# A fused attention layer on one core: the query projection with weights stationary, rotated with head dimensions on partitions, and carried through DRAM

## The chip, the core and the metric

The kernel runs on one core of a Trainium2 chip. Everything is fp32 data. The metric is device time in microseconds (us) of one execution; three runs of the kernel before gave 1683.66, 1688.36 and 1689.98 us, so the median is 1688.36.

## What is computed

One layer of a hybrid network over 1024 latent tokens and 128 context tokens, 1152 in all, with 1024 channels. Of its many parts these matter here:

```
h = rmsnorm(x, g1) * (1 + sc1) + sh1                 # 1152 x 1024
u_f, q, k, v, g = split(h @ w_in)                    # 512 | 1024 | 256 | 256 | 2048 columns
q, k = apply_rope(q), apply_rope(k)                  # latent tokens only; 16 q heads, 4 kv heads, head_dim 64
#   x1, x2 = x[..., 0::2], x[..., 1::2];  out pairs = (x1*c - x2*s, x1*s + x2*c)
scores = q k^T / 8, masked to a +/-128 token window, plus 128 cached context keys and a sink logit
attn_o = softmax(scores) v
x = x + ga1 * merge(fourier(u_f), attn_o, gates(g))  ;  then an MLP of width 4096
```

A product q.k does not change when the 64 head dimensions of both q and k are put in another common order, which is what the change makes use of.

## The kernel before

Tokens are cut into nine tiles of 128 (eight latent, one context). h lies in SBUF transposed, channels on partitions, as two fp32r parts (a rounded high part h_hi and the rest h_lo), eight slices of 128 channels each. Every projection is computed from such parts with three matmuls for each pair of slices, high*high, high*low and low*high (helper `mm3`, L193 to L195), so that the result has nearly fp32 accuracy. Weights come by DMA into a tile `wraw` and are split by ScalarE (L145, high part) and VectorE (L140, the difference).

The order of the work around the change is: the Fourier branch with gate units between its steps; then the projection of k and v for all tiles (`tok_proj_round`, L231 to L233); then the attention stage; then the rest of the layer, which the change does not touch. A **gate unit** (`gate_units`, L463) is filler: 24 matmuls of 128x384 with weights stationary and 384 tokens streaming, one of three token chunks of one of 16 blocks of 128 gate columns, 48 units in all. 16 of them run before the attention stage and 32 in it, one in most steps (`filler`, L488).

The attention stage has 36 steps, four groups g of four heads by nine token tiles i. A step s does this:

- `attention_q` (L674) for the *next* step: 24 matmuls of 128x256 into one PSUM bank `q`, with a token tile of h stationary and 256 columns of w_in streaming. So q has tokens on partitions. VectorE rotates it (`apply_rope`, L600: two products from PSUM at L602 and L605, two sums at L612 and L613) and splits it (L688). TensorE transposes the four heads (L691) into a `ptp` bank, and ScalarE copies them to `qT` (L696), where each head is 128 rows: 64 dimensions of the high part and 64 of the low part.
- `attention_scores` (L699): for each of four heads two matmuls (L712, L713), qT stationary and up to 512 keys streaming, into one of two `s` banks; VectorE masks and takes the maximum (L714); ScalarE exponentiates (L726); VectorE inverts the sum (L734); GpSimd scales (L736).
- `attention_out` (L745) for the step *before*: transposes of the probabilities (L755) into one of two `ptp` banks, a copy and a difference (L760, L140 pl), matmuls with v (L765, L766), and the sum of the two halves (L769 to L772), stored by SP (L773).

GpSimd and ScalarE also run slices of the modulation product meanwhile (L303, L305). PSUM has eight banks: two `mm` for gate units, and in this stage one `q`, two `ptp`, two `s`, one `o`. Each engine executes its queue in order; the order is fixed when the program is built, by a scheduler that works from the program order and its own estimate of times. SP issues nearly all DMAs, in order, and an issue that waits holds up those behind it.

## Time and profile before

| | |
|---|---|
| three runs, us | 1683.66, 1688.36, 1689.98 |
| span of the profiled execution, us | 1688.9 |
| mean granted TensorE clock | 0.995 |
| Fourier and k, v projection with filler gates, roughly | 140 to 246 us |
| attention stage, roughly | 246 to 707 us |
| TensorE busy in the attention stage | 441.98 of 461 us |
| VectorE, ScalarE, GpSimd busy in it | 355.67, 325.73, 206.52 us |

The profiled execution is one of its own; no time but its span is known of it, and that lies 0.5 us above the median of the three runs. A matmul's duration in the profile is from its start to its modelled end, and overlaps the next one: what a matmul takes of TensorE is the distance between the starts of two.

### The profile page before, as it was taken

To read this page: it belongs to the slowest core of one execution; us is meant where nothing else is said; L and a number is where in the kernel's file an instruction comes from. 1 tells how busy PE (TensorE), PEld (TensorE's weight loads), DVE (VectorE), ACT (ScalarE), POOL (GpSimd) and SP (SyncE) were. 2 spreads that over 40 slices of the span, in tenths; PEclk is the share of its full clock that TensorE was granted. 3 is DMA by queue.
4 is the path that set the end of the run, shared out by engine and by line. 5 is a ranking of instruction groups with operands and counts; after the bars stand their busy time and mean duration, and the time that the engine had idled before them with its cause. 6 is when DMAs were issued, how large, how long until landed. Compare 5 with 4: busy or idle time off the path is not lost.

```text
span 1688.9 us, 26480 instructions
## 1 busy us (share of the span) xinstructions
PE 1635.4 (97%) x9101; PEld 1453.2 (86%) x9101; DVE 1181.3 (70%) x2402; ACT 916.0 (54%) x1845; POOL 271.6 (16%) x368
## 2 busy tenths in 40 slices
PE   6999999999999999999999899999999999999998
PEld 5899899999899999889988788888888888888887
DVE  7663257777868787778757966777775588776764
ACT  7743236767767767655436664444443454444542
POOL 1010015444535445300001500000000200000000
PEclk9999999999999999999999999999999999999999
DMA  8341481313322211279655524445446996666751
GB/s 294 120 138 65 137 246 42 95 55 96 89 73 79 87 53 56 91 238 311 191 196 191 162 101 159 155 167 169 164 149 144 321 387 194 199 194 191 248 165 63
DMA packets 202038, 264.92 MB, mean 157 GB/s; under 512 B 29400, under 2 KB 129688, under 8 KB 201904
## 3 DMA queue, kind: packets, MB, share of 16 engines
q1 hardware_dynamic: 193648, 253.27, 46.7%
q0 software_dynamic: 8256, 9.96, 2.3%
q8 instruction: 72, 1.18, 0.3%
q14 instruction: 62, 0.51, 0.1%
HBM read 194.73 MB, written 68.44 MB: 156 GB/s over the span
## 4 chain that ended last, share of the span: by engine, by line
PE 78%; DVE 8%; ACT 4%; DMA 4%; issue 3%; POOL 1%; SPq 0%; DVEq 0%; ACTq 0%; POOLq 0%
PE x L1682 6%; PE x L1683 6%; PE x L1681 6%; PE x L1285 6%; PE x L1287 6%; PE x L1286 6%; PE mm L193 3%; PE mm L194 3%; PE mm L195 3%; PE ptp L755 2%; PE x L195 2%; PE x L194 2%; PE x L193 2%; PE x L231 1%; PE x L232 1%
## 5 line engine op out<-in xcount | busy, mean ns | idle before, releaser
L140 DVE TENSOR_TENSOR wlo<-wraw,whi 128x1024 fp32r<-128x1024 f32 x100 | 125.8, 1260 | 83.7 <-ACT whi L145 83.4
L145 ACT CAST whi<-wraw 128x1024 fp32r<-128x1024 f32 x98 | 102.5, 1050 | 97.7 <-PE x L233 20.5
L1682 PE MATMUL x<-BR 128*128 128x512 f32 (+1 forms) x348 | 132.8, 382 | 0.0
L1683 PE MATMUL x<-BR 128*128 128x512 f32 (+1 forms) x348 | 132.4, 382 | 0.0
L1681 PE MATMUL x<-BR 128*128 128x512 f32 (+1 forms) x348 | 131.3, 382 | 0.0
L736 POOL TENSOR_SCALAR pt<-pt,mx 128x512 f32<-128x512 f32 (+2 forms) x144 | 97.0, 685 | 154.6 <-DVE mx L734 137.8
L726 ACT ACTIVATE pt<-pt,mx 128x513 f32<-128x513 f32 (+2 forms) x144 | 94.7, 661 | 35.7 <-DVE mx L724 35.1
L714 DVE CUSTOM_DVE_ANT_0 pt<-s,mask,sink 128x512 f32<-128x512 f32 (+2 forms) x144 | 94.7, 672 | 23.1 <-PE ptp L755 12.4
L1654 ACT CAST BR<-aa 128x512 fp32r<-128x512 f32 x80 | 49.7, 621 | 104.9 <-issue 46.2
L140 DVE TENSOR_TENSOR pl<-ptp,ph 128x512 fp32r<-128x512 f32 (+1 forms) x136 | 86.0, 640 | 14.4 <-ACT ph L760 13.2
L305 POOL TENSOR_TENSOR macc<-macc,mprod 128x512 f32<-128x512 f32 x70 | 92.1, 1316 | 20.1 <-ACT mprod L303 20.0
L194 PE MATMUL mm<-BR,whi 128*128 128x384 f32 x272 | 92.1, 339 | 0.0
L760 ACT CAST ph<-ptp 128x512 fp32r<-128x512 f32 (+1 forms) x136 | 72.5, 546 | 32.6 <-PE ptp L755 30.9
L193 PE MATMUL mm<-BR,whi 128*128 128x384 f32 x240 | 83.6, 348 | 0.0
L1285 PE MATMUL x<-BR,whi 128*128 128x512 f32 (+2 forms) x204 | 79.2, 388 | 4.1 <-ACT ZR L1309 2.8
L195 PE MATMUL mm<-BR,wlo 128*128 128x384 f32 x240 | 81.2, 338 | 0.0
L755 PE MATMUL ptp<-ident,pt 128*128 128x128 f32 x496 | 75.9, 274 | 2.4 <-ACT qT L696 2.1
L1287 PE MATMUL x<-BR,wlo 128*128 128x512 f32 (+2 forms) x204 | 77.6, 380 | 0.0
L1286 PE MATMUL x<-BR,whi 128*128 128x512 f32 (+2 forms) x204 | 77.5, 380 | 0.0
L140 DVE TENSOR_TENSOR BR<-aa,BR 128x512 fp32r<-128x512 f32 x80 | 54.9, 687 | 31.3 <-ACT BR L1654 30.0
L1681 PEld LDWEIGHTS x<-BR 128*128 128x128 f32 x348 | 65.4, 188 | 13.1
L1682 PEld LDWEIGHTS x<-BR 128*128 128x128 f32 x348 | 65.4, 188 | 12.8
(466 smaller groups left out, 5192.9 us busy)
## 6 DMA issues: line engine op xcount, KB each, us to landing
aa<-hr_d SPq DMA_DIRECT2D x108, 256.0 KB
ab<-in_w_ff_dram SPq DMA_DIRECT2D x108, 256.0 KB
hr_d<-ZR SPq DMA_DIRECT2D x104, 256.0 KB
wraw<-in_w_in_dram SPq DMA_DIRECT2D x40, 512.0 KB
wraw<-in_w_ff_dram SPq DMA_DIRECT2D x34, 512.0 KB
mraw<-in_w_ada_dram SPq DMA_DIRECT2D x96, 128.0 KB
wraw<-in_w_out_dram SPq DMA_DIRECT2D x24, 512.0 KB
z_d<-z SPq DMA_DIRECT2D x48, 192.0 KB
```

Of the source, the lines that this page charges most:

```text
L140: eng.tensor_tensor(dst, raw, hi.bitcast(F32), ALU.subtract)
L145: nc.scalar.copy(hi, raw)
L193: nc.tensor.matmul(out, ah, bh, start=start, stop=False)
L194: nc.tensor.matmul(out, ah, bl, start=False, stop=False)
L195: return nc.tensor.matmul(out, al, bh, start=False, stop=stop).ins
L755: nc.tensor.transpose(pst[:, bi, e, :], pt[:, e, b * P : (b + 1) * P], ident)
L1285: nc.tensor.matmul(po, wh, xh, start=(k == 0 and not cont), stop=False, skip_group_check=cont)
L1286: nc.tensor.matmul(po, wh, xl, start=False, stop=False, skip_group_check=cont)
L1287: nc.tensor.matmul(po, wl, xh, start=False, stop=(k == 3), skip_group_check=cont)
L1681: nc.tensor.matmul(ps, xh, bh, start=start, stop=False, skip_group_check=cont)
L1682: nc.tensor.matmul(ps, xh, bl, start=False, stop=False, skip_group_check=cont)
L1683: nc.tensor.matmul(ps, xl, bh, start=False, stop=stop, skip_group_check=cont)
```

## The change

The q projection is turned round. The columns of w_in for q are reordered on the host so that, in each group of four heads, the 32 even dimensions of the four heads come first (128 columns, e = 0) and the 32 odd ones after them (e = 1). A **q unit** (g, j, e) has the shape of a gate unit: the 128 columns stationary, 384 tokens of chunk j streaming, 24 matmuls of 128x384. So q comes out with dimensions on partitions, and the rotation is between two PSUM results, with tables `ropet` that have dimensions on partitions: two products from the even unit, two from the odd one, a difference and a sum, then a copy (high part) and two differences (low parts). Four tiles (even high, odd high, even low, odd low) of 128x384 are stored to DRAM, and `load_qt` reads them back as `qT` for three token tiles, with even high, odd high, even low and odd low of a head below one another on 128 partitions. k is written with its even and odd dimensions in the same order (host reordering of cache_k; `even_odd` in `k_rope`).

24 q units take the place of the 36 calls of `attention_q`. The six units of group 0 run before the k, v projection; the 18 others go with the 32 gate units into one list `work`, 50 units, of which `fill` hands out an even share in each of 34 steps, after the score matmuls of the step. `qT` for a chunk is asked for three steps ahead. The `q` bank becomes a third `s` bank. The tiles of the k, v evacuation get two buffers each in a pool of their own.

```diff
+    q_d = dp.tile([NG, NJ, 4, P, CH], F32, name="q_d")
-        rope = p1.tile([P, 2, 8, HD], F32, name="rope")
-        nc.sync.dma_start(rope, rope_in)
+        ropet = p1.tile([P, 2, NT], F32, name="ropet")
+        nc.sync.dma_start(ropet, ropet_in)
+        def q_units(g):
+            blk, t = {}, {}
+            for j in range(NJ):
+                for e in range(2):
+                    def emit(j=j, e=e):
+                        if j == 0:
+                            blk[e] = load_w(w_in, 0, KC, OFF_Q + g * 256 + e * P, P)
+                        ps = mmt()
+                        gemm_unit(ps, j, wcols(blk[e], KC), hs)
+                        r = slice(j * CH, (j + 1) * CH)
+                        c, sn = ropet[:, 0, r], ropet[:, 1, r]
+                        v = ps[:, :CH]
+                        tt = nc.vector.tensor_tensor
+                        if e == 0:
+                            for n in range(2):
+                                t[n] = p1.tile([P, CH], F32, tag=f"qt{n}", name=nm("qt"), bufs=1)
+                                tt(t[n], v, (c, sn)[n], ALU.mult)
+                            return
+                        for n in range(2, 4):
+                            t[n] = p1.tile([P, CH], F32, tag=f"qt{n}", name=nm("qt"), bufs=1)
+                            tt(t[n], v, (sn, c)[n - 2], ALU.mult)
+                        tt(t[0], t[0], t[2], ALU.subtract)
+                        tt(t[1], t[1], t[3], ALU.add)
+                        for n in range(2):
+                            hi, lo = t[2 + n].bitcast(F32R), t[n].bitcast(F32R)
+                            nc.scalar.copy(hi, t[n])
+                            sub(nc.vector, lo, t[n], hi)
+                            for part, x in ((n, t[2 + n]), (2 + n, t[n])):
+                                nc.sync.dma_start(q_d[g, j, part], x)
+                    yield emit
+        for f in q_units(0):
+            f()
...
-        def attention_q(g, i, qw):
...
+        def load_qt(g, j):
+            qt = pq.tile([P, 4, CH], F32R, tag="qT", name=nm("qT"), bufs=2)
+            for part in range(4):
+                r = slice(32 * part, 32 * part + 32)
+                nc.sync.dma_start(qt.bitcast(F32)[r], q_d[g, j, part].rearrange("(h r) c -> r h c", h=4))
+            return qt
...
-                    sp = q1.tile([P, 512], F32, tag="s", name=nm("s"), bufs=2)
-                    nc.tensor.matmul(sp[:, :n], qT[:, h, :], kth[:, k0 * P : k0 * P + n], start=True, stop=False)
+                    sp = q1.tile([P, 512], F32, tag="s", name=nm("s"), bufs=3)
+                    qs = qT[:, h, (i % 3) * P : (i % 3 + 1) * P]
+                    nc.tensor.matmul(sp[:, :n], qs, kth[:, k0 * P : k0 * P + n], start=True, stop=False)
...
+        share = -(-len(gates) // NG)
+        for g in range(NG):
+            if g + 1 < NG:
+                fs = list(q_units(g + 1))
+                work += fs[:-1] + [lambda g=g + 1, f=fs[-1]: q_last(g, f)]
+            for _ in range(min(share, len(gates))):
+                work.append(gates.pop(0))
+        total = len(work)
+        def fill(s, after):
+            left = total - min(total, -(-total * s // FILL_AT))
+            with tc.issue_after(after):
+                while len(work) > left:
+                    work.pop(0)()
...
             if pending is not None:
                 attention_out(*pending)
-                if s % SKIP:
-                    filler(1, anchor)
+            fill(s, anchor)
```

Apart from numbers in names, the first 794 rows of TensorE's queue (up to the last gate unit of the Fourier branch) and the last 4165 (from the end of the attention stage on) stay in the same order; between them there are 3072 rows where there were 3397.

The first place is TensorE's queue behind the last gate unit of the Fourier branch. Before, the projection of k and v (`x` banks) follows at once:

```order
L195 MATMUL mm_239_1569<-BT_70,wlo_236_1538 128x384
L231 MATMUL x_248_1632<-whi_246_1628,BR_69 128x512
L232 MATMUL x_248_1632<-wlo_247_1629,BR_69 128x512
L233 MATMUL x_248_1632<-whi_246_1628,BR_69 128x512
L231 MATMUL x_249_1636<-whi_246_1628,BR_69 128x512
```

In the changed kernel there stand the first matmuls of the six q units of group 0 (`mm_244` to `mm_262`; each has 24 rows), and only then the k, v projection:

```order
L197 MATMUL mm_239_1570<-BT_70,wlo_236_1539 128x384
L195 MATMUL mm_244_1619<-BR_69,whi_242_1615 128x384
...
L195 MATMUL mm_250_1654<-BR_69,whi_248_1650 128x384
...
L195 MATMUL mm_253_1693<-BR_69,whi_242_1615 128x384
...
L195 MATMUL mm_262_1790<-BR_69,whi_248_1650 128x384
...
L233 MATMUL x_272_1854<-whi_270_1850,BR_69 128x512
```

144 matmuls have come ahead of the k, v projection, and their products need `ropet`, which is loaded just there.

The second place is TensorE's queue in an early step of the attention stage. Before, the 24 matmuls of the q tile (`q_481`) are laid in ones and threes between score matmuls (`s`), transposes (`ptp`) and output matmuls (`o`), and end in the transposes of q (L691):

```order
L195 MATMUL q_481_2884<-qwh_326_2167,BR_69 128x256
L712 MATMUL s_454_2762<-kth_2155,qT_402_2541 128x512
L713 MATMUL s_454_2762<-ktl_2156,qT_402_2541 128x512
L193 MATMUL q_481_2884<-qwh_326_2167,BT_70 128x256
...
L766 MATMUL o_419_2598<-pl_425_2618,vg_321_2157 128x256
...
L755 MATMUL ptp_432_2646<-ident_82,pt_371_2392 128x128 x4
...
L691 MATMUL ptp_443_2727<-identr_1602,qhl_441_2720 128x128 x4
L193 MATMUL mm_479_2856<-BR_69,whi_477_2852 128x384
```

In the changed kernel a unit (`mm_526`, a q unit) stands as one run of 24 rows, and the attention's own matmuls stand together:

```order
L727 MATMUL s_504_3046<-ktl_2392,qT_359_2421 128x512
L195 MATMUL mm_526_3137<-BR_69,whi_413_2626 128x384
...
L726 MATMUL s_531_3179<-kth_2391,qT_359_2421 128x512
L727 MATMUL s_531_3179<-ktl_2392,qT_359_2421 128x512
L769 MATMUL ptp_479_2909<-ident_83,pt_426_2698 128x128 x2
L779 MATMUL o_469_2874<-ph_471_2880,vg_354_2393 128x256
...
L769 MATMUL ptp_482_2922<-ident_83,pt_426_2698 128x128 x4
...
L779 MATMUL o_478_2908<-ph_480_2914,vg_354_2393 128x256
```

The fine mixture of filler and attention has become runs of the one and of the other.

The third place is VectorE's queue in the same stage of the changed kernel, between two q pairs: the low parts of one pair (`qt_410`, `qt_411`), then the products of the next even unit (`qt_453`, `qt_454`), which are written to the same two buffers, and behind them the drain of a score bank (L728). The waits named DMAHW are for landings of DMAs:

```order
L142 TENSOR_TENSOR qt_410_2620<-qt_410_2620,qt_416_2655 128x384 [waits Activation_49]
...
L142 TENSOR_TENSOR qt_411_2622<-qt_411_2622,qt_417_2657 128x384 [waits Activation_49]
L738 TENSOR_SCALAR mx_427_2699<-mx_427_2699 128x2 [waits DVE_49]
L748 RECIPROCAL mx_419_2670<-mx_419_2670 128x2 [waits Activation_49]
L619 TENSOR_TENSOR qt_453_2817<-mm_452_2792,ropet_1607 128x384 [waits DMAHW5_49,DVE_49,PE_49]
L748 RECIPROCAL mx_427_2699<-mx_427_2699 128x2 [waits Activation_49]
L619 TENSOR_TENSOR qt_454_2819<-mm_452_2792,ropet_1607 128x384 [waits DMAHW0_49,DVE_49]
L728 ISA pt_456_2826,mx_457_2827<-s_458_2829,mask_1605,sink8_1611 128x512 [waits PE_49,Pool_49]
```

Before, VectorE's products of q (L602) wait for TensorE alone:

```order
L602 TENSOR_TENSOR ra_400_2530<-q_397_2503,rope_1606 128x256 [waits PE_49]
L605 TENSOR_TENSOR qr_398_2528<-q_397_2503,rope_1606 128x256
L714 ISA pt_363_2363,mx_364_2364<-s_366_2370,mask_1604,sink8_1610 128x512 [waits PE_49]
L714 ISA mx_364_2364 128x1
L612 TENSOR_TENSOR qhl_399_2529<-ra_400_2530,qr_398_2528 128x4x64 [waits DVE_49]
```

So a wait of VectorE for stores to DRAM is new in this stage, with the softmax of the step queued behind it.

More of the change, by code (lines that the diff above doesn't have):

```diff
@@ L45 @@
 FILL_0 = 3
-SKIP = 14
 FILL_KV = 5
+FILL_AT = 34
 MOD_A = (2, 1)
@@ L79, in backbone_kernel @@
     rope_in: bass.AP,
+    ropet_in: bass.AP,
     dft_in: bass.AP,
@@ L615, in put_v @@
-        def put_v(src, t):
-            vv = p1.tile([P, NG, 2, HD], F32R, tag="qhl", name=nm("qhl"), bufs=2)
-            nc.scalar.copy(vv[:, :, 0, :], src)
-            sub(nc.vector, vv[:, :, 1, :], src, vv[:, :, 0, :])
-            nc.sync.dma_start(vh_d[:, t], vv.bitcast(F32))
+        def q_units(g):
[28 more added lines that the diff above has]
+                    yield emit
@@ L621, in backbone_kernel, with kv_tile, even_odd, pairs @@
+        for f in q_units(0):
+            f()
         with ExitStack() as skv:
             qk = skv.enter_context(tc.tile_pool(name="qk", bufs=6, space=PSUM))
+            pk = skv.enter_context(tc.tile_pool(name="pk", bufs=1))
+            rope = pk.tile([P, 2, 8, HD], F32, name="rope")
+            nc.sync.dma_start(rope, rope_in)
             def bankk():
                 return qk.tile([P, 512], F32, tag="x", name=nm("x"))
+            def kv_tile(tag, n, w=1):
+                shape = [P, NG, HD] if w == 1 else [P, NG, 2, HD]
+                return pk.tile(shape, F32 if w == 1 else F32R, tag=tag, name=nm(tag), bufs=n)
+            def even_odd(x):
+                return x.rearrange("p h (two d) -> p h d two", two=2)
+            def pairs(x):
+                return x.rearrange("p h (d two) -> p h d two", two=2)
+            def k_rope(dst, src, t):
+                a, b = kv_tile("ra", 2), kv_tile("rb", 2)
+                nc.vector.tensor_tensor(a, src, rope[:, 0, t, :].unsqueeze(1).to_broadcast([P, 4, HD]), ALU.mult)
+                sn = rope[:, 1, t, :].unsqueeze(1).to_broadcast([P, 4, HD])
+                nc.vector.tensor_tensor(pairs(b), pairs(src)[:, :, :, ::-1], pairs(sn), ALU.mult)
+                nc.vector.tensor_tensor(even_odd(dst), pairs(a), pairs(b), ALU.add)
+            def put_v(src, t):
+                vv = kv_tile("qhl", 2, 2)
+                nc.scalar.copy(vv[:, :, 0, :], src)
+                sub(nc.vector, vv[:, :, 1, :], src, vv[:, :, 0, :])
+                nc.sync.dma_start(vh_d[:, t], vv.bitcast(F32))
@@ L657, in backbone_kernel @@
             filler(FILL_KV, anchor)
+        pq = s1x.enter_context(tc.tile_pool(name="pq", bufs=1))
         q1 = s1x.enter_context(tc.tile_pool(name="q1", bufs=1, space=PSUM))
-        def load_q(g):
-            out = []
-            for hf in range(2):
-                raw = raw_w([P, 4, 256])
-                c0 = OFF_Q + g * 256
-                nc.sync.dma_start(raw, w_in[hf * 512 : (hf + 1) * 512, c0 : c0 + 256].rearrange("(k p) n -> p k n", p=P))
-                hi = p1.tile([P, 4, 256], F32R, tag="qwh", name=nm("qwh"), bufs=2)
-                lo = p1.tile([P, 4, 256], F32R, tag="qwl", name=nm("qwl"), bufs=2)
-                nc.scalar.copy(hi, raw)
-                sub(nc.vector, lo, raw, hi)
-                out.append((hi, lo))
-            return out
@@ L742, in attention_scores @@
                 pts.append(pt)
-            return pts
+            return pts, last.ins
         def attention_out(g, i, pts, vg):
@@ L926, in backbone_kernel @@
                 if s == len(units) - 2:
-                    filler(100, anchor)
                     load_fx()
@@ L1866, in _constants @@
     rope = np.stack([cos2, sin2], 0).reshape(2, 8, P, HD).transpose(2, 0, 1, 3).astype(np.float32)
+    ropet = np.zeros((2, HALF, NT))
+    ropet[0] = 1.0
+    ropet[:, :, :NLAT] = np.stack([c, s], 0).transpose(0, 2, 1)
+    ropet = np.tile(ropet, (1, 4, 1)).transpose(1, 0, 2).astype(np.float32)
     nrm = 1.0 / math.sqrt(1024 * 128)
@@ L1889, in _constants @@
     dftm = np.concatenate(parts, axis=1).astype(np.float32)
-    return ident, mask, np.ascontiguousarray(rope), dftm
+    return ident, mask, np.ascontiguousarray(rope), np.ascontiguousarray(ropet), dftm
 def kernel(**inputs):
@@ L1907 @@
     )
-    ident, mask, rope, dftm = _constants()
+    ident, mask, rope, ropet, dftm = _constants()
+    w_in = a["w_in"][0]
+    w_q = w_in[:, OFF_Q:OFF_KV].reshape(D, NG, QPK, HALF, 2).transpose(0, 1, 4, 2, 3).reshape(D, 1024)
     ins = {
@@ L1912 @@
         "rows": rows,
-        "cache_k": a["cache_k"].reshape(P, 4, HD),
+        "cache_k": a["cache_k"].reshape(P, 4, HALF, 2).transpose(0, 1, 3, 2).reshape(P, 4, HD),
         "cache_v": a["cache_v"].reshape(P, 4, HD),
@@ L1927 @@
         "rope": rope,
+        "ropet": ropet,
         "dft": dftm,
```

79 lines of the change are left out of this document (21 added, 58 removed).

## Prediction

> **What bounds the kernel now.** I read the page first, then stage sums, then the waits of the one stage that changes, and last single rows for prices. In the page's parts 1 and 4 (busy time and share of the span; the chain that ended last, by engine) the reader sees that TensorE (PE) is the limit:
>
> ```profile
> span 1688.9 us, 26480 instructions
> ...
> PE 1635.4 (97%) x9101; PEld 1453.2 (86%) x9101; DVE 1181.3 (70%) x2402; ACT 916.0 (54%) x1845; POOL 271.6 (16%) x368
> ...
> PE 78%; DVE 8%; ACT 4%; DMA 4%; issue 3%; POOL 1%; SPq 0%; DVEq 0%; ACTq 0%; POOLq 0%
> ```
>
> TensorE's queue is the same outside 175 to 707 us, so only the attention stage and the start of the k, v projection count. The sums over the stages (stretch, its length, then busy us of PE, PEld, DVE, ACT, POOL, the granted clock, DMA share, GB/s):
>
> ```profile
> 142.00:246.00 104.00, 104.00 (x543) 93.63 (x541) 35.12 (x67) 32.50 (x59) 7.56 (x16) 1.00 0.54 163
> 246.00:707.00 461.00, 441.98 (x3100) 422.49 (x3098) 355.67 (x967) 325.73 (x813) 206.52 (x290) 0.99 0.26 73
> ```
>
> From 142 to 246 us TensorE never rests. In the attention stage it idles 461.0 - 442.0 = 19.0 us, and VectorE is 77% busy, ScalarE 71%. What TensorE's idle waits end on there (total us, times, longest):
>
> ```profile
> PE s L712 <- DVE mx L714: 5.7, 7, 1.8
> PE o L766 <- DVE pl L140: 4.3, 4, 1.7
> PE ptp L691 <- DVE pl L140: 3.6, 4, 1.6
> PE ptp L755 <- ACT qT L696: 2.1, 1, 2.1
> PE q L193 <- DVE qr L605: 1.6, 3, 0.6
> ```
>
> All are small: the stage is bound by TensorE's own work, so work taken from it is worth nearly its full length.
>
> **TensorE's work.** Prices are distances between starts (first column us of start, second its duration). The last 23 matmuls of a q tile, then a gate unit of 24, each by the first row and the row behind the last:
>
> ```profile
> 249.91 0.28 PE L194 MATMUL q<-qwl,BR 128*128 128x256 f32 x1
> ...
> 252.64 0.46 PE L691 MATMUL ptp<-identr,qhl 128*128 128x128 f32 x4
> ```
>
> ```profile
> 224.03 0.33 PE L193 MATMUL mm<-BR,whi 128*128 128x384 f32 x1
> ...
> 228.21 0.33 PE L193 MATMUL mm<-BR,whi 128*128 128x384 f32 x1
> ```
>
> A 256-wide matmul takes 2.73 / 23 = 0.119 us, a 384-wide one 4.18 / 24 = 0.174 us. 36 x 24 = 864 of the first go, 102.8 us; 24 x 24 = 576 of the second come, 100.2 us. That saves 2.6 us. The columns streamed are the same (864 x 256 = 576 x 384), so this is only the cost per instruction: by these rows the slope is 0.055 us for 128 columns and what is left, 0.119 - 0.110 = 0.009 us, is paid 288 times less. The Trainium skill (TensorE: Matmul & The Clock Gate, Back-to-back issue gap) gives N/2.4 + 2.5 ns for matmuls apart from their weight loads, and by that rule the saving would be 94.3 - 93.6 = 0.7 us. By that rule a 256-wide matmul takes 0.109 us, where the rows here have 0.119.
>
> The transposes of q, in the run of rows where nothing waits:
>
> ```profile
> 410.95 0.46 PE L691 MATMUL ptp<-identr,qhl 128*128 128x128 f32 x4
> 411.24 0.41 PE L193 MATMUL mm<-BR,whi 128*128 128x384 f32 x1
> 411.48 0.34 PE L194 MATMUL mm<-BR,whi 128*128 128x384 f32 x1
> 411.66 0.33 PE L195 MATMUL mm<-BR,wlo 128*128 128x384 f32 x1
> ```
>
> From 410.95 to 411.66 lie four transposes and two 384-wide matmuls; 0.71 - 2 x 0.174 = 0.36 us is for the transposes. 36 x 0.36 = 13.0 us go, and nothing takes their place on TensorE, since DMA now brings q into stationary form. So 15.6 us of TensorE's work goes.
>
> **Moved work.** The six units of group 0, 6 x 4.18 = 25.1 us, go ahead of the k, v projection, from a stage with 19 us of idle time into one with none; that is neutral, unless the stage that is left lacks filler. It would have 461 - 25.1 - 15.6 = 420 us. What VectorE and ScalarE then do in it, from the stage's groups (busy us of all, then mean ns of one):
>
> ```profile
> L140 DVE TENSOR_TENSOR pl<-ptp,ph 128x512 fp32r<-128x512 f32 x109 | 74.2, 687 | 13.1 <-ACT ph L760 12.2
> ...
> L696 ACT CAST qT<-ptp 128x512 fp32r<-128x512 f32 x36 | 20.8, 579 | 7.0 <-PE ptp L691 6.9
> L140 DVE TENSOR_TENSOR qhl<-qr,qhl 128x256 fp32r<-128x256 f32 x36 | 20.7, 574 | 0.7
> ...
> L613 DVE TENSOR_TENSOR qr<-ra,qr 128x256 f32<-128x256 f32 x32 | 20.3, 634 | 0.6
> ...
> L724 DVE TENSOR_SCALAR mx<-mx 128x2 f32<-128x2 f32 x71 | 19.3, 272 | 0.6
> ...
> L612 DVE TENSOR_TENSOR qhl<-ra,qr 128x256 fp32r<-128x256 f32 x32 | 17.0, 530 | 3.7 <-PE ptp L691 3.6
> ...
> L602 DVE TENSOR_TENSOR ra<-q,rope 128x256 f32<-128x256 f32 x32 | 13.3, 416 | 3.2 <-PE q L195 3.1
> ...
> L734 DVE RECIPROCAL mx<-mx 128x2 f32<-128x2 f32 x70 | 11.2, 160 | 21.4 <-ACT pt L726 21.1
> ...
> L140 DVE TENSOR_TENSOR pl<-ptp,ph 128x256 fp32r<-128x256 f32 x20 | 8.4, 420 | 1.2 <-ACT ph L760 1.0
> ```
>
> and, from later in the kernel, the groups with a q unit's shape, 128x384, out of PSUM on VectorE and on ScalarE:
>
> ```profile
> L1006 DVE TENSOR_TENSOR z<-x,z 128x384 f32<-128x384 f32 x24 | 13.2, 550 | 0.5 <-ACT z L1005 0.5
> ...
> L993 ACT CAST ER<-z 128x384 fp32r<-128x384 f32 x21 | 10.0, 515 | 7.4 <-DMA z<-att_d 7.3
> ```
>
> VectorE loses 20.7 + 20.3 + 17.0 + 13.3 = 71.3 us, and the second product (L605), as long as the first, 13 more: 84 us. A q pair costs it eight operations of 128x384, 8 x 0.55 = 4.4 us; the nine pairs of the stage 39.6 us. 355.7 - 84 + 39.6 = 311 us of 420 is 74%. ScalarE loses 20.8 and gets 18 x 0.515 = 9.3: 314 us, 75%. GpSimd's 206.5 us are 49%. No engine overtakes TensorE, and the filler left (50 units, 209 us) is half of the stage, as before (32 gate units, 133.8, and 103 of q: 237 of 461).
>
> **Stalls that go.** `ptp` L691, q L193 and L755 after `qT` wait 3.6 + 1.6 + 2.1 = 7.3 us for steps that are no longer there, and a third score bank works against the 5.7 us. A wait ended often only uncovers the next: bounds 0 and 13.0, taken 3.5.
>
> **Stalls that come.** At the start of the q units VectorE needs `ropet`. What happens there before (z's store is the last use of the memory that the new tables take; DVE's row is the first that needs the third load):
>
> ```profile
> 174.85 0.33 PE L195 MATMUL mm<-BT,wlo 128*128 128x384 f32 x1
> ...
> 175.77 0.32 SPq L475 DMA_DIRECT2D z_d<-z  x1
> ...
> 177.71 0.30 ACT L590 CAST identr<-ident 128x128 fp32r<-128x128 f32 x1 [1.97 <-DMA z_d<-z]
> ...
> 177.82 0.33 SPq L592 DMA_DIRECT2D mask<-in_mask_dram  x1
> ...
> 178.21 0.43 SPq L594 DMA_DIRECT2D rope<-in_rope_dram  x1
> ...
> 182.78 0.18 DVE L598 TENSOR_SCALAR sink<-sink_sb 128x16 f32<-128x16 f32 x1 [15.71 <-DMA qr<-in_cache_k_dram]
> ```
>
> 904 KB (mask 384, rope 512, sink 8) need 182.78 - 177.82 = 4.96 us. `ropet` is 1152 KB in place of 512: 640 KB more, 3.5 us at that pace (904 / 4.96 = 182 KB per us), and 0 if the landing was set by latency alone. So the first product starts between 182.8 and 186.3. TensorE fills both `mm` banks by 175.0 + 2 x 4.18 = 183.4 and gets one back after two products, 1.1 us: it stands 0.5 to 4.0 us, taken 3. After that a pair's chain (eight operations 4.4, two copies 1.0, store 1.9 from 175.77 to 177.71) is 7.3 us against 8.4 us of matmuls, so the single buffers hold nothing up. The stage also opens with eight score tiles in a row and three banks, without filler: about 1 us.
>
> In the stage, VectorE's wait for the stores of a pair comes nine times. By the third place in the section on the change, VectorE does 0.69 + 0.42 + 0.55 + 0.27 + 0.16 = 2.1 us of other work between the low part `qt_410` and the product that needs that buffer, and 0.27 + 0.16 + 0.55 + 0.16 = 1.1 us after `qt_411`; issue (0.39 from mask to rope) and landing take 0.4 + 1.9 = 2.3 us. That leaves 0.2 + 1.2 = 1.4 us a pair, 13 us in all, on an engine that is idle a quarter of the time; bounds for TensorE 0 and 13, taken 2.5. SP's 36 stores and 44 loads of q in the stage (80 of some 0.4 us, 32 us in 420) and their 80 x 0.197 = 16 MB (37 GB/s on top of 73) find room.
>
> **Sum** against the profiled execution: 1688.9 - 15.6 - 3.5 + 3.0 + 1.0 + 2.5 = 1676.3; the median is 0.5 us lower, so **1675.8 us**.
>
> **Rivals.** (1) *More goes than the work.* The chain q, rotation, transpose, copy, scores was the only one that had to end within a step, so its waits go without heirs, and with three score banks those 5.7 us as well; the other terms as above. 1675.8 + 3.5 - 13.0 = 1666 us; with VectorE's wait hidden, 1664. For: the waits named. Against: `o` after `pl` remains.
>
> (2) *The gain goes into coarser filler.* q's 24 matmuls were laid in ones and threes between dependent steps; a unit now runs as one, and the transposes, outputs and scores meet in a lump. If each of 34 lumps waits 0.35 us more (the longest such waits now are 1.6 to 2.1), 12 us are back: 1688 us, no change. For: the order's second place. Against: the run of 4.2 us lies just where `pl` needs time.
>
> (3) *Slower, through VectorE's queue.* VectorE stands in order before the product until a store has landed, and the score drains behind it stand too; TensorE fills its score banks and stops. If both stores of a pair are waited out in full, 2 x 2.3 = 4.6 us, and SP issues them late behind its other waits, 3 us a pair can reach TensorE, 27 in place of 2.5: 1700 us. It decides where 9 pairs eat the other terms (15.1) and 8.4 more, from 2.6 us a pair. For: the queue's third place. Against: VectorE's 26% of idle time. [...]
>
> That the change does not do what it says is not a rival: the transposes of q are gone from the queue.
>
> **How the numbers follow.** About 0.5% (8.4 us) is what a measurement of this kernel can tell from no change. Forecast 0.46, rival 1 0.16, rival 2 0.24, rival 3 0.14. The forecast's own stretch goes half way to the bounds of the unknown terms (4.8 + 1.2 + 1.2 down, 1.8 + 0.5 + 5.2 up), 1669 to 1683, most of it under 1680; with rival 1 that gives 0.60 for faster, its upper end with rival 2 0.26 for the same, rival 3 0.14 for slower. The range leaves rival 3 out; it goes from rival 1's 1664 less the 6 us by which runs of one kernel lie apart to rival 2's 1688 and 5 more: 1658 to 1693.
>
> **What would show it.** Right: no L691 rows; 576 matmuls of q at 0.174; a PE wait of 1 to 4 us near 183 on VectorE's first product; the stage from the k, v projection's end to the f units about 420 us; idle time of TensorE in it at 13 to 20 us. Rival 2: idle time about 30 us, on `pl`, `at` and `mx`. Rival 3: VectorE idle before q's products on DMA q_d for over 25 us, and scores waiting for it. Wrong altogether: ScalarE or VectorE over 90% busy in the stage, or a change behind it.

## The result, and the profile after

Four runs of the changed kernel gave 1733.96 to 1735.67 us, median 1735.16; the kernel before took 1688.69 beside it (four runs, 1683.66 to 1689.98). The ratio is 1.0273 (1.0251 to 1.0295): 46 us slower, where the prediction said 13 us faster.

The page of the changed kernel, parts 1 and 4:

```profile
span 1733.0 us, 25745 instructions
...
PE 1640.6 (95%) x8669; PEld 1448.6 (84%) x8669; DVE 1163.2 (67%) x2334; ACT 906.6 (52%) x1826; POOL 272.2 (16%) x368
...
PE 67%; DVE 8%; DMA 3%; ACT 3%; issue 3%; POOL 1%; SPq 0%; DVEq 0%; ACTq 0%; POOLq 0%
```

TensorE has less to do and a longer span, and its share of the chain fell from 78% to 67%. From here on "the stage" is the stretch from the first score matmul to the last: 254.9 to 706.9 us before, 277.0 to 749.9 after. Its sums, first before and then after (length, busy us of PE, PEld, DVE, ACT, POOL, granted clock, DMA share, GB/s), and after them two stretches of the changed kernel:

```profile
254.90:706.90 452.00, 434.13 (x3037) 414.96 (x3035) 349.78 (x955) 321.91 (x808) 206.42 (x290) 0.99 0.25 72
```

```profile
175.00:273.00 98.00, 95.39 (x473) 85.67 (x472) 39.63 (x71) 23.32 (x39) 8.25 (x16) 0.98 0.57 165
...
273.00:400.00 127.00, 102.17 (x571) 93.68 (x570) 76.82 (x201) 72.78 (x179) 49.46 (x64) 0.91 0.40 109
...
277.00:749.90 472.90, 417.90 (x2508) 389.29 (x2508) 320.48 (x865) 309.80 (x782) 206.38 (x287) 0.96 0.37 105
```

By the forecast 41 us were to leave (25.1 moved ahead, 15.6 gone); of these 55 of q's matmuls and four transposes, some 7 us, lay ahead of this stretch already. So it was to become about 34 us shorter, and is 21 us longer. Two things fill most of that gap of 55 us. TensorE's idle time went from 452.0 - 434.1 = 17.9 us to 472.9 - 417.9 = 55.0, 37 us more. And its clock fell: 1% of 452 us is 4.5 us, 4% of 472.9 is 18.9, by this estimate about 14 us more. Before the stage nothing is amiss: 98 us from 175 to 273 are the 71 us of before, 25.1 of moved units and the wait for the tables.

What TensorE's idle time in the stage ended on (total us, times, longest; before, the score matmuls had 5.7 us in 7 waits here):

```profile
PE s L726 <- DVE mx L728: 31.0, 32, 4.8
PE ptp L769 <- DVE pl L142: 8.2, 7, 3.4
PE o L779 <- DVE at L786: 6.2, 5, 2.0
PE o L779 <- ACT mprod L305: 3.9, 1, 3.9
PE ptp L769 <- DVE ktl L142: 2.4, 1, 2.4
PE o L780 <- DVE pl L142: 2.3, 5, 0.8
```

Nearly all of it is a wait for VectorE, though VectorE is busy only 320 of 473 us: it is late at particular places. One of them, in VectorE's rows (start, duration) and then in TensorE's:

```profile
326.09 1.25 DVE L142 TENSOR_TENSOR wlo<-wraw,whi 128x1024 fp32r<-128x1024 f32 x1 [0.77 <-PE ptp L769]
327.26 0.96 DVE L142 TENSOR_TENSOR qt<-qt,qt 128x384 fp32r<-128x384 f32 x1
328.14 0.74 DVE L728 CUSTOM_DVE_ANT_0 pt<-s,mask,sink 128x512 f32<-128x512 f32 x1
```

```profile
324.76 0.39 PE L727 MATMUL s<-ktl,qT 128*128 128x512 f32 x1
...
326.26 0.60 PE L769 MATMUL ptp<-ident,pt 128*128 128x128 f32 x4
328.94 0.50 PE L726 MATMUL s<-kth,qT 128*128 128x512 f32 x1 [2.08 <-DVE mx L728]
329.28 0.40 PE L727 MATMUL s<-ktl,qT 128*128 128x512 f32 x1
329.52 0.34 PE L195 MATMUL mm<-BR,whi 128*128 128x384 f32 x1
```

Three score tiles are done by 325, all three banks are full, and their drains stand in VectorE's queue behind a weight split and a low part of q, and VectorE itself stood 0.77 us before the split. TensorE needs a bank for the fourth tile and stands 2.08 us. The run of 24 filler matmuls that could have filled this time begins at 329.52, behind the fourth tile: the filler is there, on the wrong side of the wait.

The other loss, the clock, behind a longer gap (the releaser printed in the row is one of several: the bank of `o` came free when VectorE's `at` ended at 340.04):

```profile
340.19 0.55 PE L779 MATMUL o<-ph,vg 128*128 128x256 f32 x1 [3.92 <-ACT mprod L305]
...
341.49 0.63 PE L727 MATMUL s<-ktl,qT 128*128 128x512 f32 x1
341.91 0.63 PE L726 MATMUL s<-kth,qT 128*128 128x512 f32 x1
...
351.33 0.52 PE L196 MATMUL mm<-BR,whi 128*128 128x384 f32 x1
351.65 0.52 PE L197 MATMUL mm<-BR,wlo 128*128 128x384 f32 x1
...
352.57 0.34 PE L195 MATMUL mm<-BR,whi 128*128 128x384 f32 x1
352.74 0.34 PE L196 MATMUL mm<-BR,whi 128*128 128x384 f32 x1
...
361.31 0.39 PE L726 MATMUL s<-kth,qT 128*128 128x512 f32 x1
361.54 0.39 PE L727 MATMUL s<-ktl,qT 128*128 128x512 f32 x1
```

```profile
340.00:350.00 10.00, 8.19 (x26) 6.12 (x27) 7.04 (x22) 4.97 (x13) 3.14 (x5) 0.50 0.42 134
```

A 512-wide matmul takes 341.91 - 341.49 = 0.42 us here, and 361.54 - 361.31 = 0.23 later; a 384-wide one 0.32 at 351.33 and 0.17 at 352.57, where the slow stretch has just ended. The window in it has a granted clock of 0.50.

### The profile page after: what moved, and what is told of

Same layout as the page of the kernel before. It is cut to its first block, busy times and chain, and to the rows that moved or that the text cites. A ratio compares the mean times of both kernels' runs of the same rounds, so it can differ in the third digit from the quotient of the medians.

```text
span 1733.0 us, 25745 instructions
## 1 busy us (share of the span) xinstructions
PE 1640.6 (95%) x8669; PEld 1448.6 (84%) x8669; DVE 1163.2 (67%) x2334; ACT 906.6 (52%) x1826; POOL 272.2 (16%) x368
## 4 chain that ended last, share of the span: by engine, by line
PE 67%; DVE 8%; DMA 3%; ACT 3%; issue 3%; POOL 1%; SPq 0%; DVEq 0%; ACTq 0%; POOLq 0%
PE x L1711 6%; PE x L1710 6%; PE x L1712 6%; PE x L1314 6%; PE x L1316 6%; PE x L1315 6%; PE mm L195 3%; PE mm L196 3%; PE mm L197 3%; PE x L196 2%; PE x L195 2%; PE x L197 2%; PE ptp L769 2%; DVE pt L728 2%; PE x L1147 1%
## 5 line engine op out<-in xcount | busy, mean ns | idle before, releaser
L142 DVE TENSOR_TENSOR wlo<-wraw,whi 128x1024 fp32r<-128x1024 f32 x108 | 139.3, 1291 | 100.5 <-ACT whi L147 99.5
L147 ACT CAST whi<-wraw 128x1024 fp32r<-128x1024 f32 x106 | 110.8, 1049 | 109.3 <-PE x L235 23.5
L196 PE MATMUL mm<-BR,whi 128*128 128x384 f32 x408 | 140.5, 344 | 0.0
L195 PE MATMUL mm<-BR,whi 128*128 128x384 f32 x360 | 125.2, 348 | 2.4 <-DVE qt L619 2.1
L197 PE MATMUL mm<-BR,wlo 128*128 128x384 f32 x360 | 124.0, 344 | 0.0
L728 DVE CUSTOM_DVE_ANT_0 pt<-s,mask,sink 128x512 f32<-128x512 f32 (+2 forms) x144 | 93.1, 673 | 39.3 <-PE ptp L769 33.4
L726 PE MATMUL s<-kth,qT 128*128 128x512 f32 (+2 forms) x144 | 60.8, 424 | 32.8 <-DVE mx L728 31.0
L1314 PE MATMUL x<-BR,whi 128*128 128x512 f32 (+2 forms) x204 | 79.2, 388 | 4.1 <-ACT ZR L1338 2.8
L196 PEld LDWEIGHTS mm<-BR,whi 128*128 128x128 f32 x408 | 79.5, 195 | 1.3
L779 PE MATMUL o<-ph,vg 128*128 128x256 f32 x248 | 68.0, 296 | 10.9 <-DVE at L786 6.2
L305 ACT ACTIVATE mprod<-mraw,siluc 128x256 f32<-128x256 f32 x140 | 63.7, 503 | 27.5 <-POOL macc L307 22.4
```

The source lines that it names most:

```text
L142: eng.tensor_tensor(dst, raw, hi.bitcast(F32), ALU.subtract)
L147: nc.scalar.copy(hi, raw)
L195: nc.tensor.matmul(out, ah, bh, start=start, stop=False)
L196: nc.tensor.matmul(out, ah, bl, start=False, stop=False)
L197: return nc.tensor.matmul(out, al, bh, start=False, stop=stop).ins
L728: nc.vector.tensor_tensor_reduce(out=pt[:, e, :n], in0=sp[:, :n], in1=mask[:, m0 : m0 + n], scale=1.0, scalar=sink8[:, h0 + e : h0 + e + 1 ...
```

## The experiments

Three theories came from this. **A, place**: a unit is one run of filler behind a step's scores, where q's matmuls were laid between them, so dependent work meets without cover. **B, amount**: the stage needs its filler to cover its chains, so filler moved ahead does not shorten it. **C, VectorE's lumps**: eight operations of 128x384 for a q pair delay the drains. Each result is given as a distance to the kernel before, timed on the same chip beside it; the changed kernel itself is at +46.5 us.

### Amount

The kernel before with six gate units moved to where the changed kernel has its six q units:

```diff
+            filler(6)
             vc = p1.tile([P, NG, HD], F32, tag="ra", name=nm("ra"), bufs=1)
...
-                if s % SKIP:
+                if s * 26 // 34 != (s - 1) * 26 // 34:
```

> The kernel before, with six of its 32 gate units (6 x 4.18 = 25.1 us) moved from the attention stage to the place ahead of the k, v projection, where the changed kernel has its six q units; the other 26 are spread evenly over the steps. TensorE's work is the same. Theory A (the changed kernel loses because its filler stands in one run a step, where q's matmuls were laid between the score matmuls): the fine mixture stays, so about 1689 us, at most 1695. Theory B (a step of the stage cannot become shorter than its softmax chain allows, so filler moved ahead is simply added): the stage keeps about 461 us, so 1689 + 25 = 1714 us. Theory C (VectorE's lumps of eight q operations delay the score drains): 1689 us.

Measured: 1730.38 us, +39.5, ratio 1.0228 (1.0208 to 1.0248). Its stage and its two largest waits:

```profile
281.20:743.50 462.30, 421.18 (x2893) 397.66 (x2891) 344.16 (x954) 318.97 (x803) 204.78 (x292) 0.96 0.25 67
```

```profile
PE ptp L692 <- DVE pl L140: 15.4, 9, 6.1
PE ptp L756 <- ACT qT L697: 10.4, 5, 4.5
```

The stage lost 25.1 us of work and became 10.3 us longer: idle 41.1 us in place of 17.9, clock 0.96 in place of 0.99. That is more than B asked for, and it comes without any part of the change. The waits are on other tiles than in the changed kernel: a stage short of filler lays open whatever chain it has.

The other way round, the five gate units behind the k, v projection put into the stage (`FILL_KV = 0` in the changed kernel):

> The changed kernel with the five gate units behind the k, v projection put into the list of the attention stage instead: 55 units there in place of 50, 20.9 us more. Theory A: runs stay as coarse, the stage goes from 478 to about 499 us, the time stays at 1735 us. Theory B: the stage has idle time for them and stays near 478 us, so 1735 - 21 = 1714 us, less what a gap at the end of the k, v projection costs. Theory C: 1735 us.

Measured: 1732.82 us, +42.0, ratio 1.0247 (1.0227 to 1.0268). B's number did not come, but its reason did. Two new waits stand ahead of the stage:

```profile
PE s L726 <- DMA qT<-q_d: 10.1, 1, 10.1
PE ptp L805 <- ACT rb L686: 8.1, 1, 8.1
```

These units had covered k's way to its transposes and q's first load. The stage itself went from 472.9 to 462.4 us with 20.9 us more work in it. What it gained was lost behind it, in work that the edit does not touch: from the last score matmul to the end it took 994.5 us, after the change 983.1. Most of these 11.4 us is one wait for the high part of a weight:

```profile
PE x L195 <- ACT whi L147: 7.3, 1, 7.3
```

So the next kernel keeps the cover with q's own units: only the two that the first steps need go ahead, four behind the projection, four gate units into the list ("refill"):

```diff
-        for f in q_units(0):
-            f()
+        first = list(q_units(0))
+        for f in first[:2]:
+            f()
...
-            filler(FILL_KV, anchor)
+            with tc.issue_after(anchor):
+                for f in first[2:]:
+                    f()
+            filler(1, anchor)
...
-                        if j == 0:
+                        if j == 0 or (g == 0 and j == 1):
                             blk[e] = load_w(w_in, 0, KC, OFF_Q + g * 256 + e * P, P)
```

> The changed kernel with only the first two units of q's group 0 ahead of the k, v projection; the other four stand behind it, where five gate units stood as cover, and four of those five gate units go into the list of the attention stage: 54 units there in place of 50, 16.7 us more, without losing the cover. (Two weight blocks are loaded twice for it.) If the stage cannot become shorter than the waits inside its steps allow, as the first runs say, it keeps its length and the time falls by what left the front: 1735 - 17 = 1718 us. If TensorE's work bounds the stage, as the prediction had it: 1735 us.

Measured: 1727.93 us, +37.8, ratio 1.0226 (1.0211 to 1.0242): 8.7 us of the 17. The stage began 13.2 us earlier and took 470.5 us, 2.4 less, with 16.7 us more in it; but 9.4 us were lost behind it, 6.3 of them in the same wait.

Whether TensorE's work counts at all was tried on the kernel before, with q's transposes done twice:

```diff
-            for h in range(4):
+            for h in (0, 1, 2, 3, 0, 1, 2, 3):
                 ins = nc.tensor.transpose(
```

> The kernel before with q's four transposes of a step done twice into the same bank: 36 x 0.36 = 13.0 us more TensorE work in the attention stage, the price that the prediction put on the transposes. If TensorE's work bounds the stage: 1690 + 13 = 1703 us. If the waits inside the steps bound it and the transposes lie in gaps: 1690 to 1694 us.

Measured: 1707.69 us, +17.5, ratio 1.0113 (1.0093 to 1.0132). The stage took 461.5 us, 9.5 more, for the 13.0 us of added work, and 7.2 us more were lost behind it. So work added to that stage is not hidden, and the price of the transposes is borne out roughly. With the first run this says where the kernel before stands: at a knee. More TensorE work costs about its length; less filler gains nothing, since the chains underneath come to light.

### Place

Units handed out in four pieces of six matmuls, at four places of a step ("pieces"):

```diff
-                        gemm_unit(ps, j, wcols(blk[0], KC), hs)
+                        for k in range(0, KC, KP):
+                            gemm_unit(ps, j, wcols(blk[0], KC), hs, ks=range(k, k + KP))
+                            if k + KP < KC:
+                                yield
...
+                if pr == 0:
+                    fill(s, last.ins, 1)
...
+            fill(s, anchor, 2)
             if pending is not None:
-                attention_out(*pending)
-            fill(s, anchor)
+                attention_out(*pending, s, anchor)
+            fill(s, anchor, 4)
```

> The changed kernel with each unit of the list handed out in four pieces of six matmuls, at four places of a step (behind the first pair's scores, behind the second pair's, between the two halves of the output, behind them). Same work, same VectorE and ScalarE operations. Theory A: TensorE's idle time in the stage falls from 57 us to about 20 and the stretches at half clock go with it (some 16 us), so 1735 - 37 - 16 = 1682 us, at most 1695. Theory B: over 1728 us, since the amount of filler is the same. Theory C: over 1728 us, since VectorE's queue has the same lumps.

Measured: 1712.97 us, +22.1, ratio 1.0134 (1.0115 to 1.0154). With 24 us gone, the place of the filler is a cause. But what went is mostly not the wait shown above: the scores still wait 26.9 of 31.0 us for their drains, while the waits of the transposes and of the output matmuls fell from 23.6 to 10.1 us and the clock rose from 0.96 to 0.98. A is not the only cause:

```profile
PE s L737 <- DVE mx L739: 26.9, 29, 4.6
```

Both together:

> As the kernel with the refill, and the list handed out in pieces of six matmuls at four places of a step as well. If missing filler and coarse runs are two separate losses, both gains add: 1713 - 17 = 1696 us. If they are the same loss twice, 1710 to 1713 us.

Measured: 1697.35 us, +7.2, ratio 1.0047 (1.0030 to 1.0065), as the two added up. The next run moved one gate unit ahead of the four q units behind the projection:

> As the kernel with refill and pieces, with the one gate unit behind the k, v projection put ahead of the four q units there. In that kernel TensorE stood 5.0 us at 255.6 for VectorE's first product of q, which is queued behind VectorE's work on k and v; a gate unit of 4.2 us, which needs only ScalarE, should cover that: 1697 - 4 = 1693 us, a little less if the slow matmuls behind the gap go as well. If VectorE is what is late there, it comes as late for the second bank, and the time stays at 1697 us.

Measured: 1698.98 us, +10.1, ratio 1.0061 (1.0041 to 1.0081). The 5.0 us gap before a unit's matmul went, and scores wait for their drains in its place; all waits of TensorE from 230 to 300 us:

```profile
PE s L741 <- DVE mx L743: 5.0, 2, 4.4
```

VectorE is late there, whatever stands first. Beyond that the order of the whole stage comes out anew with each edit: here it began 6.7 us earlier and took 10.3 us longer. So a few us between two such kernels are not the price of the edit alone.

The bank that q no longer needs, given to the transposes (three) and not to the scores (two):

```diff
-                    sp = q1.tile([P, 512], F32, tag="s", name=nm("s"), bufs=3)
+                    sp = q1.tile([P, 512], F32, tag="s", name=nm("s"), bufs=2)
...
-                    pst = q1.tile([P, 2, 2, P], F32, tag="ptp", name=nm("ptp"), bufs=2)
+                    pst = q1.tile([P, 2, 2, P], F32, tag="ptp", name=nm("ptp"), bufs=3)
```

> The changed kernel with nothing but that exchange: two score banks and three banks for transposes. If the use of the free bank is what loses, most of the 31 us of waits of scores for their drains go: 1735 - 20 = 1715 us. If coarse runs and missing filler are the loss, 1730 to 1740 us.

> As the kernel with the gate unit first, with two score banks and three banks for the transposes in place of three and two. TensorE's queue then has the scores in fours with filler on both sides, and the eight transposes and eight output matmuls of a step together. If the third score bank makes TensorE's queue run into VectorE's drains (17 us of waits of scores for them in the kernel with refill and pieces), these go down to the 6 us of the kernel before: 1693 - 11 = 1682 us. If VectorE's drains are late whatever the order: 1693 us or more.

Measured: the changed kernel with that alone 1717.66 us, +28.8, ratio 1.0169 (1.0142 to 1.0195), 18 us better. The number came, its reason did not: the scores still waited 27.2 us (16 waits, up to 8.1), and it was the waits of transposes and outputs that fell, from 23.6 to 9.6 us. With the mends so far the time was 1697.90 us, +9.0, ratio 1.0059 (1.0039 to 1.0079), no better than without. The longest wait left there lay in the opening, 5.2 us at 260.6 in the first score tiles. With the list handed out from the first step on (`4 * s + part` in place of `4 * s + part - 4`):

> As the kernel with three transpose banks (refill, pieces, gate first), with the list handed out from the first step on; there TensorE stood 5.2 us at 260.6 in the opening score tiles and ran at a granted clock of 0.90 from 250 to 300 us. If the opening is what is left of the loss: 1698 - 5 to 8, 1690 to 1693 us. If the last steps then lack what the first ones got: 1698 us.

Measured: 1687.12 us (12 runs), -2.6, ratio 0.9986 (0.9976 to 0.9995). Its stage and its largest waits:

```profile
256.10:696.70 440.60, 422.96 (x2633) 396.35 (x2631) 327.61 (x884) 315.04 (x795) 210.08 (x291) 1.00 0.46 123
```

```profile
PE s L741 <- DVE mx L743: 9.5, 10, 2.4
PE mm L196 <- DVE qt L630: 2.6, 1, 2.6
```

Idle time is back at 17.6 us and the clock at 1.00. Putting still more into it (`FILL_F = 1`):

> As the kernel with filler from the first step, with one gate unit less at each of the four places in the Fourier branch: 58 units in the stage in place of 54, 16.7 us. If the stage still lacks filler: 8 to 17 us less than that kernel. If TensorE's work bounds the stage now, or the Fourier branch waits without its gates: no gain or up to 10 us more.

Measured: 1701.11 us, +11.4, ratio 1.0061 (1.0045 to 1.0078). The stage took 28.2 us more for 16.7 us of units and the front became only 10.2 us shorter: on this side of the knee work is paid in full and more.

The converse of A on the kernel before, q in one run behind the scores:

```diff
+            if s + 1 < len(units):
+                with tc.issue_after(last):
+                    nxt = attention_q(g1, i1, qw)
+                anchor = nxt[1]
             if pending is not None:
                 attention_out(*pending)
```

> The converse on the kernel before: q's 24 matmuls of the next step stand behind all eight score matmuls of a step, in one run, where they were laid between the scores. Nothing else is changed: same work, same filler, same banks. If the place of the filler counts (theory A): 1710 us or more, with waits of scores for their drains in the place of 6 us. If only the amount of filler counts: 1685 to 1695 us. (It also leaves q's chain less time before the next step's scores, whose waits would carry the name of qT.)

Measured: 1875.66 us, +186.0, ratio 1.1105 (1.1090 to 1.1120). The stage, and what TensorE waited for:

```profile
253.40:890.70 637.30, 504.33 (x3072) 475.70 (x3073) 367.14 (x963) 332.70 (x813) 213.78 (x292) 0.87 0.19 52
```

```profile
PE ptp L691 <- DVE qhl L140: 117.1, 35, 4.9
```

This doesn't settle A. It is another wait than the one in question: q's transposes now stand right behind q's matmuls, so q's rotation is waited out in every step. It shows how gaps and clock go together, though: with a wait of 3.3 us a step the clock of the stage is 0.87, and the stage is 185 us longer, the whole of the loss.

### VectorE

The changed kernel without half of VectorE's operations on q. It leaves out the sums, the high copies and the low parts, so its q is not the q that is wanted; ScalarE's two copies of a pair go as well:

```diff
-                        tt(t[0], t[0], t[2], ALU.subtract)
-                        tt(t[1], t[1], t[3], ALU.add)
                         for n in range(2):
-                            hi, lo = t[2 + n].bitcast(F32R), t[n].bitcast(F32R)
-                            nc.scalar.copy(hi, t[n])
-                            sub(nc.vector, lo, t[n], hi)
```

> The changed kernel with the sums, the high copies and the low parts of q left out: the four products of a pair are stored as they are. VectorE does four operations of 128x384 a pair in place of eight, ScalarE none. Theory C: half of the idle time or more goes, 1712 us or less. Theories A and B: 1725 to 1735 us.

Measured: 1710.23 us, +19.4, ratio 1.0114 (1.0084 to 1.0144): 27 us for 27 us of VectorE's work and 9 us of ScalarE's. The stage took 443.4 us, 29.5 less, and the scores' waits fell from 31.0 to 16.8 us. The same on top of refill and pieces:

> As the kernel with refill and pieces, with the sums, the high copies and the low parts of q left out as before (VectorE's operations of a pair four in place of eight). If VectorE's lumps are a loss of their own (theory C): again some 25 us less, 1672 us. If they only cost where TensorE has no other filler in reach of its queue: 1690 us or more.

Measured: 1686.38 us, -2.5, ratio 0.9984 (0.9972 to 0.9997), 10 us for the same work. Most of that lies ahead of the stage, which began 8.3 us earlier: the 5.0 us wait for VectorE's product of q is gone there. The stage itself became 2.8 us shorter (448.6 to 445.8), and the scores' waits did not fall (17.4 us with these operations, 21.5 without). So C holds in the stage as far as the filler stands badly, and beyond that ahead of the stage; both numbers missed. How much of it is ScalarE's copies was not separated. Moving only the two sums to GpSimd brought nothing:

> As the kernel with refill and pieces, with the two sums of each q pair on GpSimd in place of VectorE, which takes 9 x (0.80 + 0.75) = 14 us off VectorE in the stage. Theory C (VectorE's lumps delay the score drains) gives about as much back as in the run without sums, copies and low parts: 10 to 14 us, 1684 us if the kernel without it gives 1696. Against it: GpSimd scales the probabilities, and two sums ahead of that in its queue delay a step; then no gain, 1696 us or more.

Measured: 1699.42 us, +9.3, ratio 1.0056 (1.0034 to 1.0079), 2 us worse than without.

### One mend taken out at a time

Last, from the kernel at -2.6 us, one mend taken out in each run:

> The kernel with filler from the first step (refill, pieces, gate first, three transpose banks), less the refill and what belongs to it: all six units of q's group 0 ahead of the k, v projection and five gate units behind it, 50 units in the stage, as in the changed kernel. If moving filler ahead is neutral once its place in the steps is right, as the prediction had it: 1687 us. If it is a loss of its own: the 15.6 us that it was between the two kernels with pieces, 1703 us.

> The kernel with filler from the first step, but with whole units, handed out behind each step's scores as in the changed kernel. If coarse runs are a loss of their own: the 30.6 us that they were between the two kernels with refill, 1718 us. If the other use of the free bank heals it too, which sets scores in fours with a unit between: 1690 to 1700 us.

> The kernel with filler from the first step, but with three score banks and two for transposes as in the changed kernel. If the bank is a loss of its own: the 17 us that it was in the changed kernel, 1704 us. If it only mattered with coarse runs, as the pair with and without it and no filler in the first step says: 1686 to 1690 us.

| kernel | median, us | ratio to before (interval) | to before, us | what the mend is worth here | alone in the changed kernel |
|---|---|---|---|---|---|
| all four | 1687.12 | 0.9986 (0.9976 to 0.9995) | -2.6 | | |
| without refill | 1707.02 | 1.0110 (1.0087 to 1.0133) | +17.2 | 19.8 | 8.7 |
| without pieces | 1713.74 | 1.0143 (1.0122 to 1.0163) | +23.9 | 26.5 | 24.4 |
| without the third transpose bank | 1710.41 | 1.0122 (1.0103 to 1.0140) | +20.5 | 23.1 | 17.7 |
| without filler in the first step | 1697.90 | 1.0059 (1.0039 to 1.0079) | +9.0 | 11.6 | not tried |

Each of the four is needed. Together they are worth 49 us; the four single ones add to 81, since one thing missing is enough to bring waits and slow clock back: TensorE idles 26.8, 36.4 and 38.7 us in the stage in the first three of these runs, in place of 17.6, at a clock of 0.97 to 0.98. The run without refill answers the question above all. It has six q units ahead of the stage in place of two, and 16.7 us less filler in it; its stage takes 443.1 us in place of 440.6 and begins 19.1 us later. With everything else in its place, filler moved ahead is still simply added.

## Why the prediction was wrong

**The step that failed** is "Moved work", with the sentence "that is neutral, unless the stage that is left lacks filler", and what it was answered with: "No engine overtakes TensorE, and the filler left (50 units, 209 us) is half of the stage, as before". A share of busy time cannot say whether a stage lacks filler. The kernel before with as much moved ahead lost 39.5 us, and the mended kernel with 16.7 us more moved ahead 19.8. The work moved was taken as neutral; what the runs showed is a stage that keeps its length or grows when filler leaves it.

**Rival 2's mechanism was there and priced too low.** It took 0.35 us for each of 34 lumps, 12 us in all. Its sign came, idle time on `mx`, `pl` and `at`, but 55.0 us in place of about 30: the scores' waits for their drains alone were 31.0 us in 32 waits, 0.97 each, up to 4.8. Pieces gave 24, 31 and 27 us back in three surroundings, in the first of them mostly not at the scores. That "the run of 4.2 us lies just where `pl` needs time" was no help: TensorE's waits for `pl` came to 10.5 us (7.9 before), and the scores stood most.

**The third score bank** was counted as a help ("works against the 5.7 us"). It let six score matmuls stand in a row; the bank's other use was worth 18 and 23 us in two surroundings, and 1 in a third. In the first the scores' waits stayed, so why it helps is not shown.

**The opening** was priced at 1 us. The first wait of the scores was 4.8 us, in a stretch whose clock was 0.91, and filler in the first step is worth 12 us. The rows show the chain behind that wait:

```profile
281.39 0.48 ACT L476 COPY z<-mm 128x384 f32<-128x384 f32 x1 [6.22 <-DMA z_d<-z]
```

```profile
282.38 0.69 DVE L142 TENSOR_TENSOR ktl<-ptp,kth 128x512 fp32r<-128x512 f32 x1 [4.17 <-ACT kth L807]
```

```profile
283.66 0.65 PE L726 MATMUL s<-kth,qT 128*128 128x512 f32 x1 [4.78 <-DVE mx L728]
```

ScalarE stood 6.22 us until a gate unit's store had landed, with the copies of k (`kth`) queued behind it; VectorE's low part of k waited for those, with the drain of a score bank behind it. SP had issued eight loads of `qT` from 264.5 to 271.9, and from 277 to 284 us the DMA share was 0.91, where the first 7 us of the stage before had 0.00. That the loads of q, which the prediction said would "find room", delayed the store is not shown: GpSimd's loads of v ran there as well, and no run separates the two.

**The clock** has no term in the sum, some 14 us by the two stage rows. With waits of at most 2.1 us the stage before ran at 0.99; the prediction did not ask what waits of 4 us would do besides lasting.

**What held.** The L691 rows are gone. TensorE waited for the tables where it was said, 2.1 us (3 predicted, 0.5 to 4.0):

```profile
184.44 0.44 PE L195 MATMUL mm<-BR,whi 128*128 128x384 f32 x1 [2.08 <-DVE qt L619]
```

Rival 3 did not come in its form: VectorE stood for stores of q three times in the stage,

```profile
DVE qt L619 <- DMA q_d<-qt: 4.7, 3, 2.7
```

and VectorE's products out of PSUM and ScalarE's copies took what was said (0.55 and 0.515), VectorE's operations from SBUF more:

```profile
L142 DVE TENSOR_TENSOR qt<-qt,qt 128x384 fp32r<-128x384 f32 x18 | 12.7, 709 | 0.1
...
L619 DVE TENSOR_TENSOR qt<-mm,ropet 128x384 f32<-128x384 f32 x18 | 9.6, 555 | 8.7 <-DMA q_d<-qt 4.7 <-PE mm L197 2.7 <-PE o L780 1.2
L623 DVE TENSOR_TENSOR qt<-mm,ropet 128x384 f32<-128x384 f32 x18 | 9.2, 551 | 3.1 <-PE mm L197 2.9
...
L624 DVE TENSOR_TENSOR qt<-qt,qt 128x384 f32<-128x384 f32 x9 | 7.2, 797 | 0.0
```

```profile
L628 ACT CAST qt<-qt 128x384 fp32r<-128x384 f32 x18 | 9.0, 510 | 5.5 <-DVE qt L624 3.1 <-DVE qt L625 1.9 <-ACT ot L784 0.5
```

VectorE's and ScalarE's sums in the stage (320 and 310 us) are near the 311 and 314 forecast; it was the length of the stage, forecast at 420 us from the end of the k, v projection's filler (273 to 751, 478 us), that was wrong. The 13.0 us of the transposes were tested only from the side of the kernel before, where doubling them cost 17.5 us, 9.5 of them in the stage.

**What stays open.** With all four mends the stage is 11.4 us shorter than before and the kernel only 2.6 us faster, against 15.6 us of work gone. In the profiled execution, the fastest of its twelve runs and 6.4 us shorter than the one before, the stage begins 1.2 us later, and 3.8 us are lost behind it, where TensorE is busy 12.7 of the 20 us from 709.8 us on at a clock of 0.66 (18.9 and 1.00 before). Why the stage did not gain more is not known. Since each edit lets the order of the stage come out anew, the worth of a single mend is known to some us at best (the exchange of banks, above all).

## What to carry to other kernels

Before independent work is taken out of a stage, ask which chains through the other engines it covers: a stage in which TensorE is 96% busy may stand at a knee, where added work costs about its length and removed filler gains nothing. Where the order of a queue changes from ones and threes to runs, price the waits by what stands ahead in the other engine's queue, not by the waits that the old order had. Which tile a freed buffer should go to could not be read from the totals of waits: here the scores waited most, and the bank was worth 18 us at the transposes. A wait of some us can cost the slow clock behind it as well.

## What the hardware showed

The half clock after a gap: behind 3.92 us without work the 512-wide matmuls took 0.42 us in place of 0.23, until about 352, nearly 12 us later, with waits of 0.5 and 1.0 us between. The Trainium skill (TensorE: Matmul & The Clock Gate, Part 1: The HAM clock gate) puts the array at half rate after an idle window of about 3.4 us and back after as much sustained work; the 3.92 us agree, and the stretch at half rate here is over three times as long as that, in work that was not unbroken. A second case is shorter: from 503.1 to 507.0 us TensorE did nothing but four transposes, the clock was 0.50 behind that, and it stayed there until 512.3, through 5.3 us of matmuls without a gap.

VectorE's sums of two SBUF tiles took 0.55 us as a rule; four of the 18 took longer, 2.38, 1.61, 1.23 and 0.94 us (duration in ns: shortest, median, longest):

```profile
L624 DVE TENSOR_TENSOR qt<-qt,qt x9: 539/555/2376, 298.3 to 611.0; 128x384 f32<-128x384 f32 x9
```

```profile
L625 DVE TENSOR_TENSOR qt<-qt,qt x9: 547/556/1610, 299.4 to 611.5; 128x384 f32<-128x384 f32 x9
```

At the one of 1.61 us GpSimd was in a sum of its own, which took longer too:

```profile
337.93 1.61 DVE L625 TENSOR_TENSOR qt<-qt,qt 128x384 f32<-128x384 f32 x1
```

```profile
336.90 2.22 POOL L307 TENSOR_TENSOR macc<-macc,mprod 128x512 f32<-128x512 f32 x1
```

Such a sum of GpSimd takes 1.33 us on average. The Trainium skill (Advanced Engine Details and Errata, GPSIMD Details) says that the two engines share a port and collide where VectorE has two SBUF inputs; these rows agree with it, and no run here separates it. The slow sum stands ahead of the `at` that ended at 340.04, and so in the gap of 3.92 us.
